# Four later places in the order and four low parts on GpSimd, in a two-layer encoder kernel

## The chip, the cores and the metric

The kernel runs on one core of one Trainium2 chip. The metric is device time in microseconds (us) for one execution of the whole program. The core has five engines that matter here: TensorE (PE, matrix products and transposes), VectorE (DVE), ScalarE (ACT), GpSimd (POOL), and SyncE (SP), which in this kernel issues nearly all DMA transfers. Each engine works through its own list of instructions in a fixed order, and waits at an instruction until the instructions of other engines that it depends on have signalled.

## The reference

A trunk of two layers works on 1024 tokens of width 1024, with 256 memory tokens beside them, all in fp32:

```python
h = rmsnorm(x, norm_gain[0])                       # layer 0
qa, ka, va, qb, kb, vb, qm, gate = split_cols(h @ w_in_even, ...)
ya = global_gqa(rope_2d(rmsnorm(qa)), rope_2d(rmsnorm(ka)), va)    # 8 heads, 2 key heads
yb = window_gqa(qb, kb, vb, sink, rel_bias)        # +-128 tokens, a sink logit per head
ym = memory_attn(qm, mk[0], mv[0])                 # 4 heads on the memory tokens
x = x + (concat(ya, yb, ym) * silu(gate)) @ w_out_even
h = rmsnorm(x, norm_gain[1])                       # layer 1
qc, kc, vc, qm, gate = split_cols(h @ w_in_odd, ...)
yc = neighborhood_attn(qc, kc, vc, rpb)            # 16 heads, window 8 x 16 on the token grid
ym = memory_attn(qm, mk[1], mv[1])
x = x + (concat(yc, ym) * silu(gate)) @ w_out_odd
return rmsnorm(x, final_norm_gain)
```

`mk[l], mv[l]` are the two halves of `rmsnorm(mem) @ w_mem_kv[l]`.

## The kernel before

**Number format.** Each fp32 operand of a product is split in a high part (`h`, `wh`, `ph`: the value rounded to the matmul's format, copied by ACT) and a low part (`l`, `wl`, `pl`: the value minus its high part, a subtraction on DVE or GpSimd). A product is then three matmuls: high·high, high·low, low·high. `wparts` does this for weights: `self.wsplit` names the engine of the high part and of the low part, where `"both"` means DVE and GpSimd in turn (`either`).

**Stages.** In order of time: *prep* (to about 145 us) projects the global heads' queries and keys with their norm and rotation, and the keys and values of both layers' memory (`project_a`, `mem_keys`, `mem_values`); *l0* (`even`, to 650) has four rounds of a global head pair (`global_pair`) with a memory head (`mem_att`), then four window pairs; *out0* (to 775) is layer 0's output projection, in two column halves with products of sums of weights and inputs (Strassen's scheme), whose ends (`done`) form x and its squares for the next norm; *front* (to 1030) is layer 1's input projection, again by seven products for each pair of 512-column groups; *l1* (`odd`, to 1370) and the last projection with the final norm follow.

**What sets the order.** The code is written stage by stage, but a scheduler decides the order of each engine's list before the run, from simulated times and from priorities (`with self.ahead("gate")` and the like put an instruction forward). `tc.issue_after(x)` keeps an instruction behind instruction `x` in that order. SP's list holds the loads and stores in the same way, so a store that waits for its data holds up the loads behind it.

**The places that the change touches.**

- `mem_values` multiplies the normalised memory with eight weight tiles of 128x512 (one for each 128 of the 1024 rows). Each tile is loaded (`wraw`), split by `wparts` (`wh`, `wl`, line 160) and used in six matmuls (line 590). For layer 1 it is called in the middle of the last loop of `project_a`, between two query units. A query unit multiplies (`pj`), normalises, rotates (DVE makes `rt`; GpSimd adds two of them to `rp`, line 887), transposes (`tr`), splits into the staging tiles `so` and stores these (`q`, `qa`).
- `even` keeps side work: `weight_sums` forms, for both output projections, sums of weight blocks on GpSimd (four additions of 128x192 per step, lines 1263 to 1266, between a load and two stores). A step is taken by `next(side, None)` in `global_pair`, each behind the normalisation of a pair of softmax rows. The buffer of these steps (tag `bias`) later takes the band table of the window attention (line 679).
- `gated` multiplies a head pair's output `yb` by its gate `sg` (DVE). For the rows 8 to 11 (memory heads) GpSimd then takes a difference of two halves (line 516), ACT a high part and DVE a low part (line 519), and the result is stored for the output projection. Behind row 11's gate on DVE stands the scaling of the window values (`with_rstd`, `vt`, line 311), which TensorE transposes next.
- `out_project` squares the eight new tiles of x on ACT (`square`). In the second column half GpSimd adds the squares of tiles 1 to 6 to a first sum (line 1366, `apart = 7`), and `done` adds the eighth with one DVE addition (line 1837), which the norm's reduction on TensorE (line 283) waits for.
- The function with line 1619's `product` does the *front*: for a pair of groups it forms `x` and `z` (products with the first-half inputs), then `y` with `t1`, `x` with `t2`, `y` with the second-half inputs, `x` with `t3` and a fresh `z` with `t4`. `x` and `y` are evicted by ACT (`P`) in between, because each bank takes two products that are wanted apart.

## Time and profile before

| quantity | value |
|---|---|
| time of three runs | 1484.65, 1488.05, 1488.3 us; median 1488.05 |
| the profiled execution's own time | 1488.39 us |
| its span | 1486.6 us |
| PE busy | 1465.6 us (99%), 8433 matmuls and transposes |
| DVE, ACT, POOL busy | 1034.8 (70%), 837.9 (56%), 642.2 us (43%) |
| HBM | 174.28 MB read, 83.89 MB written |
| share of PE in the chain that ended last | 85% |

The span runs from the first to the last recorded instruction; the execution's own time also holds what lies around it. A busy share says for what part of the span an engine had an instruction under way. The chain that ended last goes back from the last instruction, at each step to what released it. In rows of the timeline the first number is the start in us, the second the duration; `[0.55 <-DVE wl L160]` says that the engine was idle for 0.55 us before this instruction and that DVE's write of `wl` on line 160 ended that idleness. In rows of waits the numbers are the sum in us, the count and the longest. `x2` behind a row joins that many equal instructions.

### The profile page before, as it was taken

Reading aid. Unit: us, or ns where it says so; the run is one execution under the profiler, and the core shown is the slowest. Engines: PE = TensorE matmul, PEld = TensorE weight load, DVE = VectorE, ACT = ScalarE, POOL = GpSimd, SP = SyncE. Lnnn points to the kernel's source line nnn. Section 1 sums busy time; section 2 is a strip of 40 time slices with the busy share of each in tenths; the row PEclk is TensorE's granted clock in tenths of the full one; section 3 lists DMA queues with packets and bytes.
Section 4 is the critical chain, followed back from the end, with each engine's and each line's share of the span. In section 5 each row is a group of like instructions: output and inputs, shape, how many; then the busy total and the mean of one; then the engine's idle time right before and its main releaser. Section 6 shows DMA issues by size and latency. Waiting matters only on the chain.

```text
span 1486.6 us, 25518 instructions
## 1 busy us (share of the span) xinstructions
PE 1465.6 (99%) x8433; PEld 1275.1 (86%) x8433; DVE 1034.8 (70%) x2124; ACT 837.9 (56%) x1877; POOL 642.2 (43%) x767
## 2 busy tenths in 40 slices
PE   9899999999999999999999999999999999999998
PEld 8798888988888788888879887888998888888886
DVE  6687777777776578776687776654446787778674
ACT  7743665556655366655444444444446777777454
POOL 1223568556765656553450000001425556664454
PEclk9999999999999999999999999999999999999999
DMA  8966334334343524378553343567665568788834
GB/s 286 306 159 183 118 119 162 114 128 137 115 139 106 172 76 141 106 265 310 185 181 128 128 140 136 157 169 245 229 245 173 187 195 272 235 287 316 315 107 144
DMA packets 173860, 271.92 MB, mean 183 GB/s; under 512 B 15648, under 2 KB 96800, under 8 KB 172704
## 3 DMA queue, kind: packets, MB, share of 16 engines
q1 hardware_dynamic: 173296, 270.20, 56.2%
q8 instruction: 67, 1.10, 0.3%
q14 instruction: 65, 0.53, 0.1%
q10 hardware_dynamic: 432, 0.09, 0.0%
HBM read 174.28 MB, written 83.89 MB: 174 GB/s over the span
## 4 chain that ended last, share of the span: by engine, by line
PE 85%; DMA 5%; DVE 4%; issue 2%; ACT 2%; POOL 2%; SPq 0%; POOLq 0%; DVEq 0%; ACTq 0%
PE pj L242 15%; PE pj L62 11%; PE x L1619 7%; PE tr L133 6%; PE pv L1068 4%; PE y L1619 4%; PE pv L62 3%; PE s L62 3%; PE pj L1334 3%; PE tr L62 3%; PE sa L1334 2%; PE pv L1619 2%; PE sa L1035 2%; PE sa L1036 2%; PE s L1334 2%
## 5 line engine op out<-in xcount | busy, mean ns | idle before, releaser
L542 DVE TENSOR_TENSOR pl<-tr,ph 128x512 fp32r<-128x512 f32 (+2 forms) x352 | 204.1, 594 | 45.0 <-ACT ph L125 43.0
L242 PE MATMUL pj<-H,wh 128*128 128x512 f32 x704 | 233.7, 412 | 0.5 <-DVE vt L313 0.2
L125 ACT ACTIVATE ph<-tr 128x512 fp32r<-128x512 f32 (+2 forms) x352 | 176.3, 522 | 100.5 <-PE tr L133 76.4
L158 POOL TENSOR_SCALAR wh<-wraw 128x512 fp32r<-128x512 f32 x48 | 32.6, 682 | 275.9 <-PE x L1619 234.0
L125 ACT ACTIVATE wh<-wraw 128x384 fp32r<-128x384 f32 (+1 forms) x163 | 89.0, 553 | 99.4 <-DMA wraw<-w_mem 12.9
L242 PE MATMUL pj<-H,wl 128*128 128x512 f32 x352 | 139.1, 395 | 0.0
L242 PEld LDWEIGHTS pj<-H,wh 128*128 128x128 f32 x704 | 120.2, 189 | 18.3 <-POOL wh L158 1.1
L62 PE MATMUL pj<-H,wh 128*128 128x512 f32 x384 | 121.0, 396 | 0.0
L1121 POOL TENSOR_SCALAR pn<-pn,st 128x384 f32<-128x384 f32 (+1 forms) x128 | 72.4, 567 | 104.7 <-DVE st L1120 69.0
L133 PE MATMUL tr<-ident,P 128*128 128x128 f32 x752 | 115.4, 273 | 0.7 <-DVE pl L542 0.4
L1281 POOL TENSOR_TENSOR wl<-wraw,wh 128x384 fp32r<-128x384 f32 x56 | 63.2, 1130 | 91.4 <-ACT wh L125 85.6
L1119 ACT ACTIVATE pn<-pn,st 128x384 f32<-128x384 f32 (+1 forms) x128 | 75.1, 587 | 42.2 <-DVE st L1116 41.0
L133 PEld LDWEIGHTS tr<-ident,P 128*128 128x128 f32 x752 | 88.9, 140 | 9.1 <-DVE pl L542 1.4
L1041 ACT ACTIVATE P<-sa,st 128x1024 f32<-128x1024 f32 x64 | 71.5, 1117 | 35.3 <-PE tr L133 19.1
L1043 POOL TENSOR_SCALAR P<-P,st 128x1024 f32<-128x1024 f32 x64 | 74.0, 1159 | 32.3 <-DVE st L1042 32.3
L1040 DVE TENSOR_REDUCE st<-sa 128x1 f32<-128x1024 f32 x64 | 77.5, 1219 | 8.3 <-PE sa L1036 7.9
L62 PE MATMUL s<-k,q 128*128 128x384 f32 (+1 forms) x352 | 81.2, 327 | 0.0
L242 PEld LDWEIGHTS pj<-H,wl 128*128 128x128 f32 x352 | 66.2, 188 | 15.3
L62 PE MATMUL pj<-H,wl 128*128 128x512 f32 x192 | 75.6, 394 | 0.0
L160 POOL TENSOR_TENSOR wl<-wraw,wh 128x512 fp32r<-128x512 f32 x52 | 68.7, 1324 | 10.9 <-ACT wh L125 8.4
L62 PEld LDWEIGHTS pj<-H,wh 128*128 128x128 f32 x384 | 66.6, 188 | 5.4
L853 PE MATMUL pj<-ah,H 128*128 128x256 f32 x384 | 70.5, 281 | 0.0
(569 smaller groups left out, 4187.1 us busy)
## 6 DMA issues: line engine op xcount, KB each, us to landing
wraw<-w_o SPq DMA_DIRECT2D x52, 256.0 KB, 4.1
y<-yb SPq DMA_DIRECT2D x24, 512.0 KB, 3.2
wraw<-s SPq DMA_DIRECT2D x64, 192.0 KB, 3.7
wraw<-w_e SPq DMA_DIRECT2D x44, 256.0 KB, 3.2
k<-k SPq DMA_DIRECT2D x42, 256.0 KB, 5.4
s<-bias SPq DMA_DIRECT2D x56, 192.0 KB, 2.0
wq<-w_o SPq DMA_DIRECT2D x40, 256.0 KB, 3.4
y<-sg SPq DMA_DIRECT2D x18, 512.0 KB, 3.3
```

What stands on the lines that cost most here:

```text
L62: return lambda *a, **k: self.tc.keep_in_program_order(getattr(self.engine, name)(*a, **k))
L125: return self.nc.scalar.activation(out, in_, AF.Copy, scale=scale)
L133: self.turned = self.fence = self.pe.transpose(o, i, self.ident)
L242: self.pe.matmul(a[:, :n], s[:, kt % UNIT, :], m, start=(kt == 0 and i == 0), stop=(kt == KT - 1 and i == 2))
L542: self.low = nc.vector.tensor_tensor(pl[:, :n], tr[:, :n], ph[:, :n], op=OP.subtract)
L1040: nc.vector.tensor_reduce(st[:, 0:1], s, axis=AX.X, op=OP.max, negate=True)
L1041: nc.scalar.activation(pt, s, AF.Exp, bias=st[:, 0:1], accum_out=st[:, 1:2])
L1043: self.normal = nc.gpsimd.tensor_scalar(pt, pt, st[:, 2:3], 0.5, op0=OP.mult, op1=OP.mult)
L1119: nc.scalar.activation(o, o, AF.Exp, bias=st[:, 0:1], scale=-1.0, accum_out=st[:, 2:3])
L1121: self.normal = normal = nc.gpsimd.tensor_scalar(o, o, st[:, 3:4], 0.5, op0=OP.mult, op1=OP.mult)
L1334: last = nc.tensor.matmul(bank, s[:, k, :], y[3 * u + k][m][:, cols], start=start and u + k + e == 0, stop=u == 1 and k + e == 4, skip_gro ...
L1619: self.last = nc.tensor.matmul(bank, ws[s][:, k, :], b[k][m], start=start and k + i == 0, stop=k == UNIT - 1 and i == 2, skip_group_check= ...
```

## The change

Five edits. (1) In `project_a` the low parts of layer 1's memory value weights are made by DVE and GpSimd in turn. (2) The gates of the rows 3 and 11 are written down in the first round of the window pairs, and row 11's low part is kept behind `self.rooted`, the latest scaling by `with_rstd`. (3) The last side step of each `global_pair` is taken in `mem_att` instead, behind its normalisation for the second group. (4) `apart` is 6 in both column halves, so that the square of tile 6 is kept apart and `done` adds two terms on DVE. (5) In the front, the product with `t4` is kept behind the product of `x` with `t2`.

```diff
-            self.nc.vector.tensor_tensor(v(vt), v(p), rows, op=OP.mult)
+            self.rooted = self.nc.vector.tensor_tensor(v(vt), v(p), rows, op=OP.mult)
...
-    def gated(self, sg, y, dst, other=None):
+    def gated(self, sg, y, dst, other=None, behind=None):
...
-                nc.vector.tensor_tensor(l, y[:, second], h, op=OP.subtract)
+                with self.tc.issue_after(behind.ins) if behind else nullcontext():
+                    nc.vector.tensor_tensor(l, y[:, second], h, op=OP.subtract)
...
-                self.mem_norm(pt, st)
+                normal = self.mem_norm(pt, st)
+            if g:
+                with self.tc.issue_after(normal.ins):
+                    next(side, None)
...
             if q == 1:
+                self.wsplit = ("act", "both")
                 self.mem_values(w1m, mem, kvd[1], "so")()
+                self.wsplit = ("act", "dve")
...
                         scores(*todo.pop(0))
-                        with self.tc.issue_after(self.normal.ins):
-                            next(side, None)
+                        if todo:
+                            with self.tc.issue_after(self.normal.ins):
+                                next(side, None)
...
-        apart = 6 if last else 7
+        apart = 6
...
             product(x, u, t2, False)
+            crossed = self.last
...
-            product(z, unit(a22), t4)
+            u = unit(a22)
+            with tc.issue_after(crossed.ins):
+                product(z, u, t4)
...
                     if c0:
-                        self.squares = nc.vector.tensor_tensor(rows1, sums[0], sums[1], op=OP.add)
+                        nc.vector.tensor_tensor(rows1, sums[1], sums[2], op=OP.add)
+                        self.squares = nc.vector.tensor_tensor(rows1, rows1, sums[0], op=OP.add)
...
-            self.gated_rows(sg[0], j, y, yd)
+            rows = y
+            if j < 3:
+                self.gated_rows(sg[0], j, rows, yd)
...
-            self.gated_rows(sg[1], 8 + j, y, yd)
+            if j < 3:
+                self.gated_rows(sg[1], 8 + j, y, yd)
+        last = (sg[0], 3, rows), (sg[1], 11, y)
...
             if j == 0:
                 self.pull(10)
+                for g, nt, rows in last:
+                    self.gated_rows(g, nt, rows, yd, self.rooted)
```

The number of matmuls is the same. The lists of instructions differ at these places. GpSimd in prep, around layer 1's memory values, before:

```order
L887 TENSOR_TENSOR rp_1355<-rt_266_1337,rt_271_1351 128x512
L887 TENSOR_TENSOR rp_1441<-rt_277_1423,rt_282_1437 128x512
L887 TENSOR_TENSOR rp_1527<-rt_288_1509,rt_293_1523 128x512
L887 TENSOR_TENSOR rp_1649<-rt_313_1631,rt_318_1645 128x512
L887 TENSOR_TENSOR rp_1735<-rt_324_1717,rt_329_1731 128x512
L887 TENSOR_TENSOR rp_1927<-rt_365_1909,rt_370_1923 128x512
```

GpSimd at the same place, after (line 887 is now 892):

```order
L892 TENSOR_TENSOR rp_1355<-rt_266_1337,rt_271_1351 128x512
L160 TENSOR_TENSOR wl_1767<-wraw_1764,wh_1766 128x512
L160 TENSOR_TENSOR wl_1791<-wraw_1788,wh_1790 128x512
L892 TENSOR_TENSOR rp_1441<-rt_277_1423,rt_282_1437 128x512
L892 TENSOR_TENSOR rp_1527<-rt_288_1509,rt_293_1523 128x512
L160 TENSOR_TENSOR wl_1815<-wraw_1812,wh_1814 128x512
L892 TENSOR_TENSOR rp_1649<-rt_313_1631,rt_318_1645 128x512
L160 TENSOR_TENSOR wl_1839<-wraw_1836,wh_1838 128x512
L892 TENSOR_TENSOR rp_1735<-rt_324_1717,rt_329_1731 128x512
L892 TENSOR_TENSOR rp_1927<-rt_365_1909,rt_370_1923 128x512
```

Four low parts (`wl`) have come in between the rotations of the query units, two of them together. On SP, the load of the raw weights that belong to the third of them stood ahead of the stores of a query unit; before:

```order
L138 DMA wraw_1788<-w_mem 128x4x128
L914 DMA k_138<-k_138 64x1024
L138 DMA wraw_1800<-w_mem 128x4x128
L138 DMA wraw_1812<-w_mem 128x4x128
L930 DMA q_143<-so_1357 64x256
```

and after, where the first of the two pieces is the start of those stores and the second their end:

```order
L138 DMA wraw_1800<-w_mem 128x4x128
L935 DMA q_143<-so_1357 64x256
L936 DMA qa<-so_1357 64x256
L935 DMA q_143<-so_1358 64x256
L936 DMA qa<-so_1358 64x256
```

```order
L936 DMA qa<-so_1443 64x256
L935 DMA q_144<-so_1444 64x256
L936 DMA qa<-so_1444 64x256
L138 DMA wraw_1812<-w_mem 128x4x128
L138 DMA wraw_1824<-w_mem 128x4x128
```

The load `wraw_1812` has moved behind the stores of `so`. DVE at the end of the fourth round of layer 0, where `yb` is row 11 of the gate, before:

```order
L514 TENSOR_TENSOR yb_6150<-yb_6150,sg_5187 128x1024
L335 TENSOR_TENSOR q_5188<-vt_6276,q_5188 64x4x16x8
L336 TENSOR_TENSOR q_5189<-vt_6276,q_5189 64x4x16x8
L519 TENSOR_TENSOR yb_6150<-yb_6150,sg_5187 128x512
L311 TENSOR_TENSOR vt_6334<-pj_6309,rows_146 128x512
L703 ISA P_6355,st_6352<-sa_6354,bias_6350,sink_2119 128x256
```

and after:

```order
L514 TENSOR_TENSOR yb_6136<-yb_6136,sg_5187 128x1024
L335 TENSOR_TENSOR q_5188<-vt_6268,q_5188 64x4x16x8
L336 TENSOR_TENSOR q_5189<-vt_6268,q_5189 64x4x16x8
L311 TENSOR_TENSOR vt_6320<-pj_6295,rows_146 128x512
L520 TENSOR_TENSOR yb_6136<-yb_6136,sg_5187 128x512
L708 ISA P_6355,st_6352<-sa_6354,bias_6350,sink_2119 128x256
```

The scaling `vt` and the low part of `yb` have changed places; the instructions around them are as they were. TensorE in the front, where `pv` is the end of the second product with the first-half inputs, before:

```order
L1619 MATMUL pv_10475<-H_8875,wh_10492 128x512
L1619 MATMUL pv_10475<-H_8883,wh_10492 128x512
L1619 MATMUL pv_10475<-H_8875,wl_10493 128x512
L1619 MATMUL x_10521<-t_2036_10023,wh_10602 128x512
L1619 MATMUL x_10521<-t_2037_10024,wh_10602 128x512
L1619 MATMUL x_10521<-t_2036_10023,wl_10603 128x512
```

and after:

```order
L1627 MATMUL pv_10475<-H_8875,wh_10492 128x512
L1627 MATMUL pv_10475<-H_8883,wh_10492 128x512
L1627 MATMUL pv_10475<-H_8875,wl_10493 128x512
L1627 MATMUL y_10520<-H_8872,wh_10559 128x512
L1627 MATMUL y_10520<-H_8880,wh_10559 128x512
L1627 MATMUL y_10520<-H_8872,wl_10560 128x512
L1627 MATMUL y_10520<-H_8873,wh_10559 128x512
```

The product with `t4` (into a bank `x`, weights `wh_10602`) is no longer next; the second product into `y` (weights `wh_10559`) has taken its place. ACT's list is the same there before and after:

```order
L125 ACTIVATE wh_10580<-wq_10468 128x512
L125 ACTIVATE wh_10602<-wq_10469 128x512
L125 ACTIVATE P_10508<-pv_10475 128x512
L125 ACTIVATE P_10522<-y_10520 128x512
L125 ACTIVATE yb_10511<-P_10508 128x512
```

`P_10522` is the copy of `y`, which must be made before the second product into `y`.

More of the change, by code (lines that the diff above doesn't have):

```diff
@@ L529, in gated, with gated_rows @@
                 nc.sync.dma_start(dst[:, 4, :], y[:, second])
-    def gated_rows(self, sg, nt, y, yd):
+    def gated_rows(self, sg, nt, y, yd, behind=None):
         k = ROWS.index(nt)
-        self.gated(sg, y, yd[k], yd[k - 6] if k >= 6 else None)
+        self.gated(sg, y, yd[k], yd[k - 6] if k >= 6 else None, behind)
     def p_parts(self, tr, n):
@@ L613, in mem_q, with mem_att @@
         return qh, ql
-    def mem_att(self, q, kv):
+    def mem_att(self, q, kv, side):
         nc = self.nc
@@ L654, in mem_norm @@
         for b in range(i, i + nb):
-            nc.gpsimd.tensor_scalar(pt[:, b, :], pt[:, b, :], st[:, 12 + b:13 + b], 0.5, op0=OP.mult, op1=OP.mult)
+            normal = nc.gpsimd.tensor_scalar(pt[:, b, :], pt[:, b, :], st[:, 12 + b:13 + b], 0.5, op0=OP.mult, op1=OP.mult)
+        return normal
     def mem_flips(self, pt):
@@ L1928, in even @@
             self.global_pair(qa, ka[kv], va, kv, y, side)
-            self.gated_rows(sg[0], j, y, yd)
+            rows = y
+            if j < 3:
+                self.gated_rows(sg[0], j, rows, yd)
             if j == 3:
                 kb = self.k_pair(w, E_KB, True)
-            y = self.mem_att(mq, kvm)
+            y = self.mem_att(mq, kvm, side)
             if j < 3:
```

## The prediction

> **What bounds the kernel now.** I read the page first, then the waits of TensorE, then the timeline around each place that the change touches. These are the page's span, its busy times and its shares of the chain that ended last:
>
> ```profile
> span 1486.6 us, 25518 instructions
> ...
> PE 1465.6 (99%) x8433; PEld 1275.1 (86%) x8433; DVE 1034.8 (70%) x2124; ACT 837.9 (56%) x1877; POOL 642.2 (43%) x767
> ...
> PE 85%; DMA 5%; DVE 4%; issue 2%; ACT 2%; POOL 2%; SPq 0%; POOLq 0%; DVEq 0%; ACTq 0%
> ```
>
> TensorE (PE) is busy for 1465.6 of 1486.6 us, so all its idle time together is 21.0 us, and the chain runs through it for 85%. The change removes no matmul. It can therefore gain only inside these 21 us, and of them only the waits that it touches. The longest waits of TensorE, and the one window that gives the pace of undisturbed matmuls:
>
> ```profile
> PE tr L62 <- DVE pl L542: 2.1, 3, 1.4
> ...
> PE pj L590 <- DVE wl L160: 1.0, 3, 0.6
> PE tr L133 <- DVE vt L311: 0.8, 1, 0.8
> ```
>
> ```profile
> 975.00:1000.00 25.00, 25.00 (x109) 1.00 0.60 167
> ```
>
> The reader is to see two things. The largest wait (2.1 us) is not one that the change aims at; of those it aims at, the largest are 1.0 and 0.8. And 109 matmuls of 512 columns fit in 25.00 us, a pitch of 0.229 us, at a granted clock of 1.00, while a single row is listed with some 0.39. A listed wait costs its idle time and, as I estimate, 0.27 more: a listed matmul overlaps the next by 0.39 − 0.229 = 0.16, and the first behind a wait lasts 0.50 and not 0.39 (113.31 below), 0.11 more.
>
> The profiled execution took 1488.39 us, 1.8 above its span and 0.34 above the median, 1488.05. The sum is made against 1488.39, and 0.34 is taken off at the end.
>
> **Memory value weights (100 to 122 us).** For the second layer's memory values, eight low parts (wl = raw weight minus its high part) are made. Four of them, those of tiles 1, 3, 5 and 7, go from VectorE (DVE) to GpSimd (POOL). The rows there, and the groups of the two GpSimd operations in 95 to 145 us:
>
> ```profile
> 113.31 0.50 PE L590 MATMUL pj<-wl,q 128*128 128x512 f32 x1 [0.55 <-DVE wl L160]
> ...
> 115.75 0.39 PE L590 MATMUL pj<-wh,mem 128*128 128x512 f32 x1
> 117.28 0.71 PE L590 MATMUL pj<-wh,q 128*128 128x512 f32 x2
> ```
>
> ```profile
> 111.78 1.48 DVE L160 TENSOR_TENSOR wl<-wraw,wh 128x512 fp32r<-128x512 f32 x1
> ...
> 113.26 0.68 DVE L160 TENSOR_TENSOR wl<-wraw,wh 128x512 fp32r<-128x512 f32 x1
> ...
> 111.44 1.27 POOL L887 TENSOR_TENSOR rp<-rt,rt 128x512 f32<-128x512 f32 x1 [2.32 <-PE tr L133]
> ...
> 112.58 1.17 SPq L138 DMA_DIRECT2D wraw<-w_mem  x2
> ```
>
> ```profile
> L887 POOL TENSOR_TENSOR rp<-rt,rt 128x512 f32<-128x512 f32 x8 | 11.1, 1382 | 36.0 <-DVE rt L884 19.4 <-DVE iq_t L783 12.8 <-PE tr L133 2.3
> L160 POOL TENSOR_TENSOR wl<-wraw,wh 128x512 fp32r<-128x512 f32 x2 | 2.5, 1288 | 0.0
> ```
>
> From the page's list of DMA issues, the last column is the time from issue to landing, in us:
>
> ```profile
> wraw<-w_e SPq DMA_DIRECT2D x44, 256.0 KB, 3.2
> ```
>
> One low part costs DVE 0.68 and GpSimd 1.29. DVE is given back 4 × 0.68 = 2.7 us of the stage. What ended last in before were three waits for DVE's low parts: 0.99 idle + 3 × 0.27 = 1.8 us. That is the most that can be gained (−1.8). The order shows what comes in their place. The load of tile 5's raw weights is no longer issued ahead of the sixteen stores of a rotated q unit on SP's queue but behind them, next to the load at 112.58. Issued about 112.2, it lands 3.2 us later, at 115.4; ScalarE's (ACT) copy of the high part follows at about 116.3 and GpSimd's low part at about 117.6. TensorE has other projections ahead of that tile now (17 rows further down), and reaches the place where it stood idle or did other work, 115.75 to 117.28, with the tile just ready or some tenths late. So the stall moves from tiles 4, 6 and 7 to tiles 5 and 7. I take −0.2, near the no-gain end because the load, not the subtraction, ends the wait. The bad end is two low parts arriving a whole GpSimd duration late, 2 × 1.29 = +2.6. The rotations (rp) that queue behind the low parts on GpSimd are hidden by its idle 36.0 us ahead of them; if that cover is gone, each is late by up to 1.29.
>
> The row at 111.78 also shows a price. That DVE subtraction took 1.48 instead of 0.68, while GpSimd's addition ran until 112.71: it got through 0.55 after that. The Trainium skill ("SBUF — State Buffer", section "Who interferes with whom") has a rule that speaks against the change: a VectorE instruction with two SBUF inputs and a GpSimd instruction that reads SBUF share a port pair, and the one behind is blocked for the whole instruction. The trace agrees here, with 1.48 against 0.68; by that rule alone the four new parts would each block VectorE up to once, and the term would lie near the loss that the slower rival below prices.
>
> **Squares (774 us).** For the second half of the first output projection, GpSimd adds one square fewer (L1366) and DVE adds two terms where it added one (L1837).
>
> ```profile
> 773.85 0.63 ACT L1364 ACTIVATE ph<-yb 128x512 f32<-128x512 f32 x1 [0.89 <-DVE yb L1359]
> 774.05 1.30 POOL L1366 TENSOR_TENSOR vt<-vt,ph 128x512 f32<-128x512 f32 x1
> 775.39 0.69 DVE L1837 TENSOR_TENSOR rows<-vt,ph 128x512 f32<-128x512 f32 x1 [1.63 <-POOL vt L1366]
> 776.22 1.02 PE L283 MATMUL pv<-inv_d,rows 128*128 128x1 f32 x8 [0.38 <-DVE rows L1837]
> ```
>
> Before, 1.30 on GpSimd is followed by 0.69 on DVE, ending at 776.08. After, the last square ends at 774.48, and two additions of 0.69 by 775.9, with 0.1 less by overlap: 775.8. TensorE's wait of 0.38 falls by 0.3. Term −0.3; it can't gain more than 0.38 and a little of the restart (−0.5), nor lose, since DVE had idled 1.63 before (0).
>
> **Last gate (502 us).** The low part of row 11's gate goes behind the first scaling of the value projection (vt) on DVE.
>
> ```profile
> 501.45 0.39 PE L242 MATMUL pj<-H,wl 128*128 128x512 f32 x1
> 503.26 0.66 PE L133 MATMUL tr<-ident,vt 128*128 128x128 f32 x4 [0.83 <-DVE vt L311]
> ...
> 501.92 0.69 DVE L519 TENSOR_TENSOR yb<-yb,sg 128x512 fp32r<-128x512 f32 x1 [1.18 <-POOL sg L516]
> 502.52 0.68 DVE L311 TENSOR_TENSOR vt<-pj,rows 128x512 f32<-128x512 f32 x1
> 503.12 0.48 DVE L703 CUSTOM_DVE_ANT_0 P<-sa,bias,sink 128x256 f32<-128x256 f32 x1
> ```
>
> The low part waited 1.18 for GpSimd's difference, with vt queued behind it. Now vt starts when its projection ends, 501.45 + 0.39 = 501.84, about 501.9 instead of 502.52: TensorE goes on 0.6 earlier. Term −0.6; −1.0 if the wait of 0.83 vanishes with its restart, 0 if something else holds vt. The low part comes 0.6 later; its reader is a store for the output projection, 150 us on, so nobody waits. The windowed softmax (L703) behind both still starts at 503.12, since the two before it take the same time together.
>
> **Weight sums (from 159 to 485 us).** The last of each head group's side steps (four GpSimd additions of 128x192, two loads or stores) goes from the global attention to behind the memory attention's normalisation.
>
> ```profile
> 209.29 0.66 PE L133 MATMUL tr<-ident,P 128*128 128x128 f32 x4 [0.40 <-DVE pl L542]
> 232.33 0.60 PE L133 MATMUL tr<-ident,P 128*128 128x128 f32 x4
> ...
> 207.08 1.55 DVE L438 SCALAR_TENSOR_TENSOR sg<-sg,vt 128x512 f32<-128x512 f32 x1
> ...
> 225.16 1.13 POOL L1043 TENSOR_SCALAR P<-P,st 128x1024 f32<-128x1024 f32 x1
> ...
> 469.59 0.37 SPq L679 DMA_DIRECT2D bias<-band  x1
> ...
> L1263 POOL TENSOR_TENSOR bias<-bias x28: 589/598/607, 159.8 to 464.9; 128x192 f32<-128x192 f32 x28
> ```
>
> The additions are the same in number. In the order GpSimd's rows at 207 us shift, so that the DVE instruction of 1.55 us (207.08), behind which TensorE waits 0.40 at 209.29, stands beside other work: 0.40 + 0.27 = 0.67 at best, of which I take half, −0.3 (bound −0.6). Three of the sums now stand ahead of one softmax normalisation (225.16), which TensorE reads at 232.33, after some 6 us of slack: 3 × 0.60 = 1.8 are hidden there, and +1.8 is the loss if that slack is gone. The band table shares the sums' buffer; its load goes from 469.59 to about 484, against a first use at 503.12, 19 us away: nothing.
>
> **Front product (893 us).** In layer 1's input projection, built from seven products for each pair of column groups, the last product (with t4, in a fresh bank that the trace calls x too) may no longer be issued ahead of the product of x with t2. Before, it stood directly behind pv's product and filled the time until y's bank was free; now the second product into y stands there, and it overwrites a bank that ACT must first have copied out.
>
> ```profile
> 893.17 0.39 PE L1619 MATMUL pv<-H,wl 128*128 128x512 f32 x1
> 894.05 0.72 PE L1619 MATMUL x<-t,wh 128*128 128x512 f32 x2 [0.49 <-ACT wh L125]
> 895.11 0.62 PE L1619 MATMUL x<-t,wh 128*128 128x512 f32 x2
> 914.38 0.73 PE L1619 MATMUL x<-t,wh 128*128 128x512 f32 x2 [0.21 <-DVE P L1651]
> ...
> 893.37 0.63 ACT L125 ACTIVATE wh<-wq 128x512 fp32r<-128x512 f32 x1 [2.10 <-PE pv L1619]
> 893.90 0.58 ACT L125 ACTIVATE P<-pv 128x512 f32<-128x512 f32 x1
> 894.38 0.59 ACT L125 ACTIVATE P<-y 128x512 f32<-128x512 f32 x1
> ```
>
> Before: the matmul at 895.11 is the fourth behind 893.17, so without a wait it would start at 893.17 + 4 × 0.229 = 894.09; the loss is 1.0. After: ACT's three instructions keep their order (wh of t4's weights, copy of pv, copy of y). The copy of y ends at 894.38 + 0.59 = 894.97, and TensorE can go on at 895.02 where it would at 893.40: a loss of 1.6, so +0.6. Later, at 914.38, the wait of 0.21 + 0.27 goes by half, −0.2, since x is then freed earlier. Term +0.4. The good end is −1.0, all of the old loss gone, if ACT's wh no longer has to wait for pv; the bad end is the new 1.6 with the restart that ACT's rows don't show, +1.2, less nothing at 914.
>
> **The sum.** −0.2 − 0.3 − 0.6 − 0.3 + 0.4 = −1.0 us: 1487.4 for an execution like the one profiled, 1487.1 against the median. All good ends together give −1.8 − 0.5 − 1.0 − 0.6 − 1.0 = −4.9, 1483.2.
>
> **The rivals.** *The waits only change place, no net change:* the front's new wait eats what the gate and the squares give, and the low parts come as late as before: +1.2 − 0.6 − 0.3 + 0 to +1.0, 1488.0 to 1489.5. For it speaks that every wait has a second one close behind (117.28, 894.97); against it, that the gate's gain hangs on nothing else. *Faster:* the three parts' stalls all vanish, the wait at 914.38 too: 1.8 + 0.5 + 1.0 + 1.0 + 0.5 + 0.67 = 5.5, 1482.6. Against it speaks the order at 893 us, where a longer wait is visible. *Slower:* the low parts on GpSimd become the path in the stage of 100 to 122 us. Each takes 1.29, DVE's own low part of the next tile and the rotations stand blocked for as long (as at 111.78), and four of them, each with a restart, cost 4 × (1.29 + 0.27) = 6.2; with the other four terms (−0.8), 1493.5. It decides when tile 5's low part ends later than about 117.4, where TensorE wants it; at my 117.6 it costs tenths. Against it: GpSimd's idle 36.0 us there, and that only two of the four have a late load.
>
> **How the numbers follow.** A measurement of this kernel tells some 0.3% from no change (the three runs span 3.65 us), that is 4.5 us. The forecast 1487.1 has a chance of 0.50 and the no-net-change rival 0.27; both lie within 0.3%: 0.77. Faster by more: 0.12. Slower by more: 0.11. The range goes from all good ends, 1483.2, to the front's bad end with one low part late, −0.3 − 0.6 − 0.3 + 1.2 + 1.56 = +1.6 on 1488.05, rounded up to 1490.0; the two outer rivals stay out of it, most of 0.2.
>
> **What would show it.** Right: a wait of about 1.4 us at 893 us by a product on y for ACT's copy P; the wait for vt at 503 down to about 0.2; the wait for the squares' rows below 0.1; none at 209 us; at 115 to 121 us waits of tenths that name GpSimd's wl in place of DVE's. Wrong: waits over 1 us each for GpSimd's wl or for rp (slower), no wait at all at 893 us (faster), or a new wait at a place that the change does not touch, by the shifted loads on SP's queue. A difference over 5 us either way would mean that I looked at the wrong places.

## The result, and the profile after

| | median, us | runs |
|---|---|---|
| kernel before | 1487.74 | 16 (1483.62 to 1491.9) |
| changed kernel | 1491.47 | 16 (1487.2 to 1495.18) |

The ratio is 1.0027, with a 95% interval of 1.0017 to 1.0038: the change makes the kernel about 4 us slower. Forecast were 1487.1 and a range up to 1490.0. Three runs among those of the experiments, one each of three kernels, took 2400 to 5100 us and are left out of the medians below. The profiled execution of the changed kernel took 1487.2 us, the shortest of its 16, so it shows the places but not the typical sum. Its span, busy times and chain:

```profile
span 1485.3 us, 25521 instructions
...
PE 1465.5 (99%) x8433; PEld 1274.8 (86%) x8433; DVE 1034.8 (70%) x2121; ACT 839.1 (56%) x1877; POOL 650.1 (44%) x770
...
PE 86%; DMA 5%; DVE 4%; ACT 2%; issue 2%; SPq 1%; POOL 1%; POOLq 0%; DVEq 0%; ACTq 0%
```

GpSimd is busy 8 us longer, and TensorE's work is the same. TensorE's waits there (sum, count, longest):

```profile
PE y L1627 <- ACT P L125: 1.5, 1, 1.5
...
PE pj L242 <- ACT wh L125: 0.9, 1, 0.9
...
PE sa L1042 <- ACT P L1048: 0.7, 1, 0.7
PE pv L283 <- DVE rows L1849: 0.7, 1, 0.7
PE sa L704 <- DVE st L708: 0.6, 2, 0.3
...
PE pj L591 <- POOL wl L160: 0.3, 1, 0.3
...
PE tr L133 <- DVE vt L311: 0.2, 1, 0.2
```

The first and the last stand where the prediction had them: the front's new wait, and the gate's wait down from 0.83. The wait for GpSimd's low parts is only 0.3. But three of the others are new and lie at places that the change does not touch: 0.9 for a high part of query weights at 133 us, 0.7 for a softmax row at 155, 0.6 for line 708 at 624 us.

One execution against one says little here, since the start alone (0 to 100 us) varies by more than 4 us. TensorE has the same 8433 rows in all these kernels, so they can be matched one to one, and the time between two of its rows compared stage by stage. The numbers are us above the kernel "no memory edit" of the experiments (the places are its times); "late sink" is explained there.

```
stage          without the memory edit            with it                             with it, late sink
(us)           before late-b sums   late-n best   changed again no-sums no-front only late  neg
131.5-143.5    -0.01  -0.01  -0.01  0.00  -0.01   1.15   0.00   1.06    0.66   0.67   0.24  0.21
143.5-160      -0.02   0.01   0.07 -0.05   0.19   1.25   1.99   2.11    3.92   3.78   0.02  0.17
215-226         0.00   2.01   0.00  0.00   0.00   0.00   0.00   3.10    0.00   1.92   0.00  0.00
370-385        -0.01  -0.02   0.48  0.19  -0.02   0.87   0.29   0.00    0.83  -0.02   0.70  0.67
495-503         0.63   0.67   0.11  0.00   0.00   0.28   0.31   0.00   -0.12   0.70   0.31  0.00
622-627         0.00   0.03   0.01  0.00   0.01   0.49   0.49   0.50    0.49   0.50   0.49  0.49
760-774         0.07   0.09   0.07  0.26  -0.02   0.34   0.35   0.34    0.35   0.07   1.08  0.35
880-920        -0.23  -0.30  -0.23  0.04  -0.23   0.00   0.00   0.00   -0.29  -0.30  -0.07  0.00
```

### The profile page after: what moved, and what is told of

The parts are those of the page before. It is cut to its first block, busy times and chain, and to the rows that moved or that the text cites. A ratio compares the mean times of both kernels' runs of the same rounds, so it can differ in the third digit from the quotient of the medians.

```text
span 1485.3 us, 25521 instructions
## 1 busy us (share of the span) xinstructions
PE 1465.5 (99%) x8433; PEld 1274.8 (86%) x8433; DVE 1034.8 (70%) x2121; ACT 839.1 (56%) x1877; POOL 650.1 (44%) x770
## 4 chain that ended last, share of the span: by engine, by line
PE 86%; DMA 5%; DVE 4%; ACT 2%; issue 2%; SPq 1%; POOL 1%; POOLq 0%; DVEq 0%; ACTq 0%
PE pj L242 15%; PE pj L62 11%; PE x L1627 7%; PE tr L133 5%; PE pv L1076 4%; PE y L1627 4%; PE pv L62 3%; PE s L62 3%; PE pj L1342 3%; PE sa L1342 3%; PE tr L62 3%; PE pv L1627 2%; PE tr L1342 2%; PE s L1342 2%; PE sa L1042 2%; PE sa L1043 2%
## 5 line engine op out<-in xcount | busy, mean ns | idle before, releaser
L160 POOL TENSOR_TENSOR wl<-wraw,wh 128x512 fp32r<-128x512 f32 x56 | 76.0, 1360 | 15.3 <-ACT wh L125 12.5
```

Source lines behind the costliest of these rows:

```text
L160: e.tensor_tensor(lf, raw, hf, op=OP.subtract)
```

## The experiments

**Which part costs it.** Three kernels undo one part each, and the changed kernel stands beside them ("again").

```diff
# no memory edit:
-                self.wsplit = ("act", "both")
                 self.mem_values(w1m, mem, kvd[1], "so")()
-                self.wsplit = ("act", "dve")
```

```diff
# no weight-sums edit: the last side step in global_pair again
-                        if todo:
-                            with self.tc.issue_after(self.normal.ins):
-                                next(side, None)
+                        with self.tc.issue_after(self.normal.ins):
+                            next(side, None)
# and the step in mem_att out; no front rule:
-            with tc.issue_after(crossed.ins):
-                product(z, u, t4)
+            product(z, u, t4)
```

> The changed kernel once more, to have a second profiled execution. Theory M (the moved loads of the memory value weights and of the query weights behind them, in 100 to 145 us, cost what the comparison shows): near 1491.5 us, about 4 us above the kernel before, and TensorE's waits between 100 and 145 us sum to 4 us more than before's there. Theory S (the moved weight sums hold up softmax rows on GpSimd): the same time, but the extra waits lie between 150 and 480 us. Theory F (the front's new order): the extra waits lie at 890 to 920 us, and are 1.5 us at most.

> The changed kernel with all low parts of layer 1's memory value weights on DVE again, the other four edits kept. M: 1487.5 us, as the kernel before or 0.5 below. S and F: 1491.5, no different from the changed kernel.

> The changed kernel with the side steps of the weight sums at their old places, the other four edits kept. S: 1487.5 us. M and F: 1491.5, no different from the changed kernel.

> The changed kernel without the rule that keeps the product with t4 behind the product of x with t2, the other four edits kept. F: 1490 us, 1.5 below the changed kernel, with no wait above 0.5 at 894 us. M and S: within 0.6 us of the changed kernel.

| kernel | median, us | ratio to before (95%) |
|---|---|---|
| changed, again | 1491.63 | 1.0022 (1.0009 to 1.0035) |
| no memory edit | 1485.34 | 0.9986 (0.9973 to 0.9998) |
| no weight-sums edit | 1493.51 | 1.0036 (1.0023 to 1.0049) |
| no front rule | 1491.62 | 1.0028 (1.0013 to 1.0042) |

The kernel before ran beside each series of experiments, and each ratio is to its runs there. Its medians lie between 1485.4 and 1487.0, so medians of two series can differ by up to 1.6 us without a cause in the kernels.

The memory edit costs 6.2 us (1491.5 less 1485.3; 5.4 by the ratios). The other four together gain some 1.5, the front's rule is worth nothing that the times can tell, and undoing the weight sums makes it worse. So theory M names the right edit, and S and F fall. But M has the wrong place: it expected 4 us more of waits between 100 and 145 us, and the row 131.5 to 143.5 has 0 to 1.15. The largest loss by the edit lies between 143 and 160 us: 1.2 to 3.9 us in the four executions here that have it, 0.2 at most where it is out. These are SP's and ACT's and then DVE's rows there in the kernel before:

```profile
144.12 1.59 SPq L138 DMA_DIRECT2D wraw<-w_e  x2
...
146.74 0.34 ACTq L1914 DMA_DIRECT2D sink<-sink_b  x1
...
148.40 1.11 ACT L1041 ACTIVATE P<-sa,st 128x1024 f32<-128x1024 f32 x1
...
150.03 1.02 DVE L1915 TENSOR_SCALAR sink<-sink 128x8 f32<-128x8 f32 x1 [0.22 <-DMA sink<-sink_b]
...
152.25 0.69 DVE L313 TENSOR_TENSOR vt<-pj,rows 128x512 f32<-128x512 f32 x1 [1.14 <-PE pj L242]
```

and the same in the changed kernel's second execution, with TensorE's behind them:

```profile
146.71 1.59 SPq L138 DMA_DIRECT2D wraw<-w_e  x2
...
147.28 1.11 ACT L1048 ACTIVATE P<-sa,st 128x1024 f32<-128x1024 f32 x1 [0.69 <-DVE st L1047]
...
151.03 0.37 ACTq L1926 DMA_DIRECT2D sink<-sink_b  x1
151.44 1.12 ACT L1048 ACTIVATE P<-sa,st 128x1024 f32<-128x1024 f32 x1 [2.96 <-DMA wraw<-w_e]
...
154.80 0.17 DVE L1927 TENSOR_SCALAR sink<-sink 128x8 f32<-128x8 f32 x1 [1.95 <-DMA sink<-sink_b]
154.88 0.68 DVE L313 TENSOR_TENSOR vt<-pj,rows 128x512 f32<-128x512 f32 x1
...
155.62 0.73 PE L242 MATMUL pj<-H,wh 128*128 128x512 f32 x2 [0.62 <-DVE vt L313]
...
157.99 0.50 PE L1042 MATMUL sa<-k,q 128*128 128x512 f32 x1 [0.71 <-ACT P L1048]
```

`sink` holds eight numbers, the sink logits that the window attention needs 350 us later. ACT issues their load, DVE negates them. The load waits on ACT's queue until a load of query weights (`w_e`) has landed, of which it reads nothing. The trace's semaphores (the signals that instructions wait for) show why: in the changed kernel the sink load waits for semaphore 103 and signals 103 itself, and the second of the two weight loads at 146.71, issued at 147.96, signals 103 too. In before the shared semaphore is 102, that of the first of the two.

Before, the sink load went at 146.74, it stood ahead of the first softmax row, and DVE waited 0.22. With the memory edit the weight loads are issued later. Their order among the stores is the same; what they wait for is a buffer that GpSimd frees with the low parts of earlier query weights. SP's waits there and GpSimd's rows, before:

```profile
SPq L138 <- POOL wl L160: 2.2, 2, 1.4
...
141.64 1.20 POOL L158 TENSOR_SCALAR wh<-wraw 128x512 fp32r<-128x512 f32 x2
142.81 2.54 POOL L160 TENSOR_TENSOR wl<-wraw,wh 128x512 fp32r<-128x512 f32 x2
```

and in the changed kernel's second execution:

```profile
SPq L138 <- POOL wl L160: 3.4, 2, 2.6
...
143.63 1.79 POOL L158 TENSOR_SCALAR wh<-wraw 128x512 fp32r<-128x512 f32 x3
145.39 3.79 POOL L160 TENSOR_TENSOR wl<-wraw,wh 128x512 fp32r<-128x512 f32 x3
```

TensorE passes the row of 143.5 us within 0.1 us at the same time in both executions. But GpSimd begins 2.0 later and makes three high parts in a row where it made two, so its first low part starts 2.6 later (145.39 against 142.81), and so does the load (146.71 against 144.12). The order also puts the sink load behind the first softmax row: it goes at 151.03, DVE stands still for 1.95 at an instruction that nobody needs yet, and behind it stand `vt`, for which TensorE waits, and the next rows.

**Is it the sink load?** The load and the negation were moved to layer 0's second round; every other row of each engine keeps its place. Once in the changed kernel, once in the kernel before, once without the memory edit, and once the negation alone in the changed kernel.

```diff
-        nc.scalar.dma_start(sink, self.io["sink_b"].to_broadcast([128, 8]))
-        nc.vector.tensor_scalar(sink, sink, -1.0, None, op0=OP.mult)
...
             self.global_pair(qa, ka[kv], va, kv, y, side)
+            if j == 1:
+                with self.tc.issue_after(self.expd.ins):     # ACT's latest exponential
+                    nc.scalar.dma_start(sink, self.io["sink_b"].to_broadcast([128, 8]))
+                with self.tc.issue_after(self.maxed.ins):    # DVE's latest row maximum
+                    nc.vector.tensor_scalar(sink, sink, -1.0, None, op0=OP.mult)
```

> The changed kernel with one small thing moved: the load of the sink logits (8 values, on ACT's queue) and their negation on DVE go from the start of layer 0 (150 us) to its second round; every other row of every engine stays where it is. Theory L (the low parts on GpSimd are harmless, but with them the sink load comes behind the first softmax row on ACT and waits there for a load of query weights; ACT's second softmax row, DVE's scaling vt and TensorE stand behind it): 3.5 to 5.5 us below the changed kernel, 1486 to 1488, and the loss between the first and the third softmax row (148 to 154 us) is gone. Theory G (the low parts or the moved weight loads themselves cost the time): no more than 1 us below the changed kernel, near 1491.

> The kernel before with the same move of the sink load and its negation. L: there the load stood ahead of the first softmax row and cost DVE only 0.22 us of waiting and 1.02 of work, and no wait of TensorE: within 1 us of the kernel before. G: the same, 0 to -1.

> The changed kernel without the memory edit and with the sink load moved, a candidate for the fastest. L: 1484.5 to 1485.3, as without the move, and within 1.5 us of the changed kernel with the sink load moved. G: 4 us or more below that kernel.

> The changed kernel with the negation of the sink logits alone moved to the second round; the load stays on ACT behind the first softmax row. If DVE's wait for the load is what counts: 1486 to 1488, as with both moved. If ACT's own wait ahead of its second softmax row counts as well: 1489 to 1490.5, between that and the changed kernel. If neither: 1491.5.

| kernel | median, us | ratio to before (95%) |
|---|---|---|
| changed, late sink | 1489.09 | 1.0014 (1.0001 to 1.0027) |
| before, late sink | 1489.54 | 1.0006 (0.9991 to 1.0022) |
| no memory edit, late sink | 1486.41 | 0.9990 (0.9977 to 1.0002) |
| changed, negation alone late | 1488.86 | 1.0010 (0.9997 to 1.0023) |

The loss at 143.5 to 160 us is gone in both changed kernels (0.02 and 0.17 in the table), and the medians fall by 2.4 and 2.6 us (from 1491.5). By the ratios it is 1.2 and 1.8 us (1.0022 less 1.0014 and 1.0010), and the intervals overlap: that the sink load costs something is shown by the stage, not by the time. The negation alone does as much as both: what counts is DVE's wait, not ACT's (its 1488.86 falls between the two ranges expected for it). In the kernel with both moved, `vt` waits for TensorE again as before, and the two softmax rows follow each other:

```profile
146.26 1.12 ACT L1048 ACTIVATE P<-sa,st 128x1024 f32<-128x1024 f32 x1 [0.70 <-DVE st L1047]
...
147.39 1.12 ACT L1048 ACTIVATE P<-sa,st 128x1024 f32<-128x1024 f32 x1
...
151.37 0.69 DVE L313 TENSOR_TENSOR vt<-pj,rows 128x512 f32<-128x512 f32 x1 [2.58 <-PE pj L242]
```

So theory L is shown for the stage, but it explains 2.5 of 6.2 us (the stage's mean loss was 2.6 in five executions and is 0.1 now): 3.5 to 5.5 were expected, and against the kernel without the memory edit and with the late sink (1486.41) 2.7 us remain. Theory L had 1.5 at most there, theory G 4 or more; neither is met. Where the sink load had done no harm, moving it brought nothing (1.0006 for before, and a median 1.1 us higher without the memory edit, both within their intervals).

A part of the remainder is the query weights themselves. In before, SP issued the pair of loads for the last memory query unit at 113.85; in the changed kernel the second of the pair goes at 128.36, behind all stores of two query units, and ACT and TensorE wait for it:

```profile
113.85 0.92 SPq L138 DMA_DIRECT2D wraw<-w_e  x2
```

```profile
128.36 0.52 SPq L138 DMA_DIRECT2D wraw<-w_e  x1
...
132.60 0.63 ACT L125 ACTIVATE wh<-wraw 128x512 fp32r<-128x512 f32 x1 [2.08 <-DMA wraw<-w_e]
...
133.29 1.19 PE L242 MATMUL pj<-H,wh 128*128 128x512 f32 x4 [0.88 <-ACT wh L125]
```

The row 131.5 to 143.5 of the table has 0 to 1.15 us for it, 0.6 in the mean of seven executions, never without the edit. No experiment gave these weights their old place back.

**Each part alone, and a candidate.** The kernel before with the memory edit alone or the weight sums alone, and the changed kernel without the memory edit and without the front's rule (diffs as above).

> The kernel before with the memory edit alone (four low parts of layer 1's memory value weights on GpSimd). If the edit costs what its removal from the changed kernel gave back: 4.5 to 6.5 us above the kernel before, 1491.5 to 1493.5, with 1 to 4 us lost between 143 and 160 us at the sink load. If the loss needs the other edits beside it: within 1.5 us of the kernel before.

> The kernel before with the moved weight sums alone. In two of three executions without that edit 2 to 4 us are lost at 215 to 240 us, in none with it. If that is what the edit is worth: 1 to 2.5 us below the kernel before, 1484.5 to 1486. If it gains only the 0.67 of the prediction's bound: 1486.2 or above.

> The changed kernel without the memory edit and without the front's rule, a candidate for the fastest: the weight sums, the last gate and the squares alone. From the stages of the executions so far the front's rule costs 0.2 to 0.3 us: 1485.1, 0.2 below the kernel without the memory edit, and 1.5 to 2 below the kernel before.

| kernel | median, us | ratio to before (95%) |
|---|---|---|
| memory edit alone | 1493.92 | 1.0051 (1.0031 to 1.0071) |
| weight sums alone | 1487.17 | 1.0009 (0.9995 to 1.0024) |
| no memory edit, no front rule | 1486.46 | 1.0001 (0.9986 to 1.0016) |

The memory edit needs no partner: alone it costs 0.31 to 0.71%, with 3.78 us at the sink load. The candidate is no better than the kernel without the memory edit alone, which stays the fastest by its ratio of all that were run, though the intervals of its two relatives overlap with its own. The weight sums alone gained nothing in the time, while undoing them in the changed kernel cost 1.9 us. The stage shows what they do: without the edit, three of four executions lose 1.9 to 3.1 us at 215 to 226 us (row 215-226), with it none of nine. Here is that place in the kernel without the weight-sums edit, GpSimd's last sum, its normalisation of four memory rows, DVE's gate beside it, TensorE, and a window of the latter's clock (the last but two number):

```profile
223.26 0.60 POOL L1270 TENSOR_TENSOR bias<-bias 128x192 f32<-128x192 f32 x1
...
224.93 2.81 POOL L656 TENSOR_SCALAR P<-P,st 128x256 f32<-128x256 f32 x4
...
224.21 1.83 DVE L514 TENSOR_TENSOR yb<-yb,sg 128x1024 f32<-128x1024 f32 x1
...
226.44 1.84 PE L133 MATMUL tr<-ident,P 128*128 128x128 f32 x4 [1.54 <-POOL P L656]
...
228.00:230.00 2.00, 2.00 (x6) 1.61 (x6) 0.69 (x1) 1.11 (x2) 1.92 (x3) 0.50 0.46 142
```

The sums stand ahead of the normalisation that TensorE's transposes need, and the edit puts them behind it. That alone is not the loss: in before's profiled execution the sums end at the same distance and nothing waits. In the three executions that lose, one of the four normalisations takes 1.44 or 1.45 us and not 0.48, and DVE's gate multiplication (`yb` by `sg`) runs beside it; in before it ran 2.5 us later than the first of them, at 225.83, and all four took 0.48. The 3.10 of the execution shown also holds a fall of the granted clock to 0.50 for 3.4 us; the other two, without one, lose 2.01 and 1.92. What the average execution gains by that is left open by times that disagree.

**The small later losses.** In all seven executions with the memory edit TensorE loses 0.49 us at 622 to 627 us, in none without it, although every engine's order there is the same. DVE's rows without the edit, and with it (where TensorE's two waits follow):

```profile
622.39 0.18 DVE L721 RECIPROCAL st<-st 128x4 f32<-128x4 f32 x1 [0.78 <-ACT P L719]
622.78 0.62 DVE L708 CUSTOM_DVE_ANT_0 P<-sa,bias,sink 128x384 f32<-128x384 f32 x1 [0.21 <-PE sa L705]
```

```profile
622.88 0.18 DVE L721 RECIPROCAL st<-st 128x4 f32<-128x4 f32 x1 [0.78 <-ACT P L719]
623.63 0.62 DVE L708 CUSTOM_DVE_ANT_0 P<-sa,bias,sink 128x384 f32<-128x384 f32 x1 [0.58 <-POOL P L726]
...
624.31 0.44 PE L704 MATMUL sa<-k,q 128*128 128x384 f32 x1 [0.29 <-DVE st L708]
...
625.65 0.44 PE L704 MATMUL sa<-k,q 128*128 128x384 f32 x1 [0.28 <-DVE st L708]
```

DVE has idled 0.37 longer behind the same instruction. The page lists a queue that carries the program itself:

```profile
q14 instruction: 65, 0.53, 0.1%
```

These are 65 transfers of 8 KB. One starts at 624.39 us in the changed kernel, when 1092 instructions of DVE's list have started (with those of its sequencer); without the memory edit it comes at 619.72, at instruction 1089. DVE's list is eight shorter with the edit (2909 against 2917), so the same fetch falls eight instructions later in the work: on a row that TensorE waits for. The transfer starts 0.76 after the late row (623.63), so DVE does not wait for this transfer's data; what it does in the 0.37 no row shows. To test it, eight tiny instructions were given back to DVE, later also eight to GpSimd in the kernel without the memory edit.

```diff
+        idle = self.st("idle", [128, 8], pool=self.base)      # 32 bytes a partition; 64 in the second series: [128, 16]
...
             self.global_pair(qa, ka[kv], va, kv, y, side)
+            if j == 1:
+                with self.tc.issue_after(self.maxed.ins):
+                    for i in range(8):
+                        nc.vector.memset(idle[:, i:i + 1], 0.0)
```

> The changed kernel with eight tiny DVE instructions (a memset of one column each) added in layer 0's second round, nothing else moved. Theory P (the small later losses, at 624 and 775 us, come from the place at which DVE fetches the next block of its program, which lies eight instructions later in the changed kernel than without the memory edit; the eight bring it back): the two waits of TensorE for line 708 at 624 us (0.29 and 0.28) are gone and the wait for the squares' rows falls from 0.67 to 0.3 or 0.4; the time falls by 0.5 to 1 us, to about 1490.8. If those losses have another cause in the memory edit: both waits stay, and the time is as the changed kernel's, 1491.5.

> The padded kernel once more (the changed kernel with eight tiny DVE instructions). If the uniform slowness of its first execution came from elsewhere: 1490 to 1491, and the stretch from 785 to 860 us takes as long as in the changed kernel. If the padding slows the kernel: again 1495 or more, with that stretch 0.4 us longer.

> The changed kernel with the sink load moved to the second round and eight tiny DVE instructions behind it. Theory P: 0.8 us below the kernel with the moved sink load, 1488.2, with no loss at 622 to 627 us; what is left above the kernel without the memory edit is GpSimd's share at 370 to 385 us and the late query weights at 133 us. If the rest is something else: 1489.1, with the loss at 622 us gone all the same.

> The changed kernel without the memory edit, with eight tiny GpSimd instructions added in layer 0's first round, nothing else moved. Theory P for GpSimd: a loss of 0.3 to 0.9 us appears at 370 to 385 us, where the kernel without them loses at most 0.2 and the changed kernel loses that much; the time rises by about as much, to 1486. If the loss there has another cause: none appears, 1485.3.

> The changed kernel with eight tiny DVE instructions in layer 0's second round, and a tile of 64 instead of 32 bytes for them; no row of any engine differs from the padded kernel. If the shift by 32 bytes made the padded kernel slow: the stretch from 785 to 860 us takes as long as in the changed kernel, the time is 1490 to 1491, and the loss at 622 to 627 us stays away. If any added tile or the instructions make it slow: 1498 again.

> The changed kernel with the sink load moved, eight tiny DVE instructions and a tile of 64 bytes. Shift theory with theory P: 1488.2, 0.8 below the kernel with the sink load moved alone. Otherwise 1493, as with the tile of 32 bytes.

> The changed kernel without the memory edit, with eight tiny GpSimd instructions in layer 0's first round and a tile of 64 bytes. Shift theory with theory P: 1485.3 to 1486, with a loss of 0.3 to 0.9 us at 370 to 385 us; the execution with 32 bytes showed 0.22 there, most of it its general slowness, which speaks against such a loss. Otherwise 1492.

| kernel | tile | median, us | ratio to before (95%) |
|---|---|---|---|
| changed, 8 for DVE | 32 bytes | 1498.76 | 1.0090 (1.0061 to 1.0119) |
| the same again | 32 | 1498.04 | 1.0083 (1.0068 to 1.0099) |
| changed, late sink, 8 for DVE | 32 | 1493.08 | 1.0057 (1.0040 to 1.0074) |
| no memory edit, 8 for GpSimd | 32 | 1492.17 | 1.0046 (1.0029 to 1.0063) |
| changed, 8 for DVE | 64 | 1495.26 | 1.0066 (1.0051 to 1.0080) |
| changed, late sink, 8 for DVE | 64 | 1492.90 | 1.0042 (1.0028 to 1.0056) |
| no memory edit, 8 for GpSimd | 64 | 1491.04 | 1.0032 (1.0017 to 1.0046) |

Four executions with the eight DVE instructions (the changed kernel twice with 32 bytes, the late sink with 32 and with 64) lose 0.02 to 0.03 us at 622 to 627 instead of 0.49, and −0.02 to 0.03 at 760 to 774 instead of 0.35, and the fetch is at instruction 1089 again in those with 32 bytes. So the place in DVE's list is shown to count, with one reservation: the tile was not tried in the changed kernel without the instructions. In the repeated kernel:

```profile
628.02 0.18 DVE L721 RECIPROCAL st<-st 128x4 f32<-128x4 f32 x1 [0.78 <-ACT P L719]
628.42 0.62 DVE L708 CUSTOM_DVE_ANT_0 P<-sa,bias,sink 128x384 f32<-128x384 f32 x1 [0.22 <-PE sa L705]
```

For GpSimd it falls: eight instructions more there bring 0.22 and 0.10 at 370 to 385 us, most of it general slowness, and not the 0.3 to 0.9 expected. That loss (0.3 to 0.9 where the memory edit and the weight sums are both in, at most 0.2 where either is out, but 0.48 once with the sums alone) stays unexplained.

Every one of these kernels is slower as a whole, by 4 to 7 us against its counterpart (4 to 10 by the ratios). The eight instructions don't do it: TensorE's pace is lower from 80 us on, ahead of them. From 920 to 1000 us, where TensorE hardly waits, the four executions with the 32-byte tile take 0.65 to 0.66 us more than the kernel without the memory edit, the two with 64 bytes 0.33 both, and of the twelve other executions without the tile all but one 0.01 at most (that one 0.33). The granted clock is 0.997 or 0.998 in all six. So with a tile of 32 bytes TensorE is slower by about 0.8% in such a stage, with one of 64 by half of that: the second series' expectation, no slowness at 64, was wrong. That the tile shifts the later tiles in memory, and that this is the cause, is argued and not shown: the traces hold no addresses, and the one execution without a new tile that has the same 0.33 (no memory edit, late sink) speaks against it as the only cause.

## Why the prediction was wrong

- **Memory value weights: the step that failed.** The term was −0.2, its bad end +2.6; measured is +6.2. What was priced, the subtractions and the waits at 100 to 122 us, is not where the time went: waits of some tenths change place, 0.3 of them for GpSimd's low parts, and TensorE takes about as long from 100 to 131.5 us with the edit (−0.6 to 1.5 against the kernel without it) as without (−0.8 to 0.6). What was put at nothing is what the moved loads and GpSimd's later work do behind that stage. The working followed one load (tile 5's) to the end of its stage and left out the second that moves, the query weights' from 113.85 to 128.36. It also left out GpSimd's work behind the stage, which comes 2.6 later at 143 us (why it begins 2.0 later there was not followed further): the weight loads that wait for its buffers, the sink load on ACT that waits for one of these, the DVE instruction behind it, and TensorE behind that. The prediction had named such a wait as a sign of being wrong ("a new wait at a place that the change does not touch, by the shifted loads on SP's queue"), without a price or a chance. The stages have 2.5 us for the sink load and 0.8 for DVE's fetch places at 624 and 775 us, both moved by an experiment, and 0.6 for the query weights, read from their wait alone; some 0.5 at 370 to 385 us are located, not explained. That leaves about 2 us which no stage shows apart from the scatter of the start and of the end (from 1000 us on the executions differ by up to 3.8 us with and without the edit), and their cause stays open.
- **The slower rival had the size (6.2 us for these weights) by luck, and not the mechanism.** GpSimd's parts are not the path: TensorE waited 0.3 for them. The port rule of the Trainium skill ("SBUF — State Buffer", "Who interferes with whom") pointed at the right side, and the trace agrees with it in the changed kernel too. GpSimd's low part at 115.02 took 1.81 instead of 1.29 beside DVE's at 115.01 (0.68), and then DVE's next instruction, a tiny one at 115.61, took 1.24 instead of 0.15, until GpSimd's part had ended at 116.83. But TensorE lost nothing there that the scatter of 100 to 131.5 us lets see.
- **Last gate: right.** TensorE's wait fell from 0.83 to 0.19 (row below), and the stage 495 to 503 from 0.63 to 0.70 in three of the four executions without the edit (0.11 in one) to between −0.12 and 0.31.
- **Front: right.** A wait of "about 1.4" was forecast for ACT's copy `P`, 1.46 is there, and the wait at 914 us is gone altogether; the stage is 0.23 longer than before (forecast +0.4). Both rows:

```profile
502.50 0.66 PE L133 MATMUL tr<-ident,vt 128*128 128x128 f32 x4 [0.19 <-DVE vt L311]
...
894.50 0.72 PE L1627 MATMUL y<-H,wh 128*128 128x512 f32 x2 [1.46 <-ACT P L125]
```

- **Squares: mis-sized.** Forecast −0.3. Without the memory edit TensorE's wait fell by 0.07 only (0.38 to 0.31), and the stage by 0.1 in two of three executions; in the changed kernel the wait rose to 0.67. The two additions were to overlap by 0.1. Instead the second started 0.11 after the end of the first without the memory edit, and 0.46 after it in the changed kernel, where DVE's next fetch place falls there:

```profile
773.69 0.69 DVE L1848 TENSOR_TENSOR rows<-ph,ph 128x512 f32<-128x512 f32 x1 [0.76 <-ACT ph L1372]
774.84 0.69 DVE L1849 TENSOR_TENSOR rows<-rows,vt 128x512 f32<-128x512 f32 x1 [0.46 <-DVE rows L1848]
...
775.68 1.02 PE L283 MATMUL pv<-inv_d,rows 128*128 128x1 f32 x8 [0.67 <-DVE rows L1849]
```

- **Weight sums: the wrong place.** The term of −0.3 was put on the wait at 209 us. That wait is gone in both executions of the changed kernel, but it is 0.53 without the memory edit, where the weight sums are the same. The edit acts at 215 to 226 us, on a normalisation that in before's profiled execution happened to be in time; one execution doesn't show a wait that comes in three of four.
- **The sum of the other four** was −0.8, and the kernel without the memory edit is 1.5 us below before (0.0002 to 0.0027 of the time): right within the interval, in part by luck, since the weight sums act at another place than forecast. The candidate with three of these edits (1.0001) does not confirm a gain.

## What to carry to other kernels

When work moves to an engine that finishes later, follow the buffers that it frees to the loads that reuse them, and each of these loads to everything that stands behind it in any queue, until the end of the next stage; a load that lands in time in the old order says nothing about the new. Put an instruction that waits for a small, early load (here eight numbers, needed 350 us later) where its engine has nothing behind it. And match the rows of the busiest engine between several executions stage by stage: a loss of half a microsecond that always sits at the same row is visible there, when the medians need a dozen runs to tell 0.2%.

## What the hardware showed that was not expected

- Where DVE fetches the next 8 KB of its program, a row started 0.37 us late at 624 us and 0.35 late at 775; if the row there is one that TensorE waits for, TensorE pays. Eight instructions more or fewer hundreds of microseconds earlier move it: 0.49 us of TensorE's time at 624 us, 0.35 at 775. On GpSimd eight instructions moved nothing that could be seen.
- Kernels with a small tile added among the long-lived ones, 32 or 64 bytes a partition, had TensorE slower by about 0.8% or 0.4% in stages without waits, and were slower by 4 to 7 us, as much as the dearest edit of this case. Why is open.
- A DMA issue on one engine's queue can wait for the landing of another engine's load of which it reads nothing (the sink's at 151.03, for `w_e`), where both signal the same semaphore (103).
- A GpSimd normalisation of 0.48 us took 1.44 or 1.45 in three executions in which DVE's multiplication of two tiles ran beside it.
